# One layer of a hybrid decoder on one core: the opening projection unit with one root per pair of row tiles, and its weight split, scaling, products and clearing in a new order

## The chip, the cores and the metric

The kernel runs on one core of a Trainium2 chip. Its engines work side by side, each through its own instructions in order: PE (TensorE, matrix products), with PEld for its weight loads, DVE (VectorE), ACT (ScalarE), POOL (GpSimd) and SP, which here only issues DMAs. The metric is the device time of one execution in microseconds (us), lower is better. Times of a trace are counted from the start of the profiled span.

## The reference, cut to what matters

```python
def reference(x, mem, ...):
    h = rms_norm(x, attn_norm[l])          # x: 512 rows of 1024, each divided by its root mean square
    proj = h @ w_in[l]                     # split into q, k, v, RWKV columns, memory q
    o_da = diff_attention(...)
    o_rw = rwkv7_time_mix(...)
    o_mem = memory_attention(...)
    x = x + concatenate([o_da, o_rw, o_mem]) @ w_out[l]
    xn = rms_norm(x, ffn_norm[l])
    return x + hierarchical_moe(xn, ...)   # 16 experts, two for each row

def rms_norm(x, gain, eps=1e-6):
    return x * rsqrt(mean(x * x, axis=-1, keepdims=True) + eps) * gain
```

The change touches only `rms_norm(x)` and the first 256 columns of `h @ w_in` (the LoRA columns of the RWKV group).

## The kernel before, in words

The 512 rows of x lie in four tiles of 128 rows, `xt[0]` to `xt[3]`; the first two are the halves of one buffer (`f_96` in lists of the order, `f` in the trace), the last two of another (`f_97`). The opening is done in two halves `hf` of 256 rows, one pair of tiles each:

- *Roots.* `row_root` sums a tile's squares for each row, on DVE (line 280, for tiles 0 and 2) or on ACT (line 282, for tiles 1 and 3; the sum is read out by a second short instruction), then POOL takes mean plus epsilon (line 283) and the power -1/2 (line 284). The squares themselves go to the scratch tiles `aw0` and `aw1`.
- *Scaling.* `half_scale` multiplies the pair by its roots: ACT takes the even tile in two pieces of 512 columns (line 355), DVE the odd one (line 356).
- *Transposes.* `half_turn(n)` turns block k of 128 columns of both tiles on PE into half of a PSUM bank (line 329). There are 16, n = 0 to 7 for the first half. Banks are shared: n = 6 and 7 use the second halves of the banks of n = 0 and 1.
- *Splits.* `half_split(n)` makes of the turned block a rounded part `hm_h` on ACT (line 292) and the remainder `hm_l` on DVE (line 293).
- *Weights.* The 256 columns come in two slots of 512 KB, `raw_79` and `raw_82`. `weights()` lets the next one be split in the same way: `whi` on ACT (line 97), `wlo` on DVE (line 98).
- *Products.* `half_products(hf, ks)` does for each block k and each of two column groups three products of 256 columns: `hm_h` by `whi`, `hm_l` by `whi`, `hm_h` by `wlo` (lines 342 to 344). A half has 48.

ACT, DVE and PE run these in the order in which the code stands (`manual_schedule`). POOL and SP do not: a scheduler places their instructions. What must not come early is put behind `later()`, which ties it to the instruction `rooted`: the clearing of a scratch tile and its DMA into spare rows of the output (lines 394, 395; the scratch tile is `aw1` again), and the clearing of `v_t`, `gm` and a mask `ob` (lines 414, 568, 584). POOL also computes distances of positions (line 897 on), for which SP loads two lists, `pown` and `posc`. After the unit PE goes on with `cols_unit`, the next projections.

Of the kernel before, what the change touches and what calls it, by code (L numbers as in the profile page):

```python
# [10 lines left out]
F32 = mybir.dt.float32  # L11
# [3 lines left out]
AF = mybir.ActivationFunctionType  # L15
ALU = mybir.AluOpType
# [4 lines left out]
P = 128  # L21
S = 512
D = 1024
NT = S // P
KC = D // P
# [6 lines left out]
RMS_EPS = 1e-6  # L32
# [119 lines left out]
def hybrid_layer_kernel(ctx, tc, x, mem, positions, cols, w_in, w_kv, w_out, wa2, g2, ffn, wr, br,  # L152
                        wg, wu, wd, out):
    nc = tc.nc
    V, A, G, T = nc.vector, nc.scalar, nc.gpsimd, nc.tensor
# [4 lines left out]
    wk = ctx.enter_context(tc.tile_pool(name="wk", bufs=2))  # L160
# [14 lines left out]
    def pc():  # L175
        return pools["ps"].tile([P, 512], F32, name="pc", bufs=2)
# [18 lines left out]
    def b4(name, shape, dtype=F32):  # L195
        return biga.tile(shape, dtype, name=name)
# [4 lines left out]
    xt = [xs[t // 2][:, t % 2, :] for t in range(NT)]  # L201
# [36 lines left out]
    mhalf = const.tile([P, 1], F32, name="mhalf")  # L238
# [31 lines left out]
    h_hi = hm.tile([P, KC, S], F32R, name="hm_h")  # L270
    h_lo = hm.tile([P, KC, S], F32R, name="hm_l")
# [4 lines left out]
    def row_root(src, vec=True):  # L276
        ss = wk.tile([P, 1], F32, name="ssx", bufs=4)
        r = wk.tile([P, 1], F32, name="rsx", bufs=4)
        if vec:
            V.tensor_tensor_reduce(b4("aw0", [P, D]), src, src, 1.0, 0.0, op0=ALU.mult, op1=ALU.add, accum_out=ss)  # L280
        else:
            A.activation(b4("aw1", [P, D]), src, AF.Square, accum_out=ss)
        G.tensor_scalar(r, ss, 1.0 / D, RMS_EPS, op0=ALU.mult, op1=ALU.add)
        return r, G.tensor_tensor(r, r, mhalf, op=ALU.pow)

    def row_scale(src):
        r, rooted = row_root(src)
        A.activation(src, src, AF.Copy, scale=r)
        return rooted

    def split_cols(ps, g, hi, lo):
        first = A.activation(hi, ps, AF.Copy, scale=g)
        return first, V.scalar_tensor_tensor(lo, ps, g, hi.bitcast(F32), op0=ALU.mult, op1=ALU.subtract)
# [19 lines left out]
    def weights():  # L313
        ws.pair.append(held.pop())
        ws.pump()
        first_w.append(ws.use())
# [3 lines left out]
    def half_bank(n):  # L320
        if n % 12 < 6 and len(banks) <= n // 12 * 6 + n % 6:
            banks.append((pt, pt, pc, pc, pp, pp)[n % 6]())
        return banks[n // 12 * 6 + n % 6][:, n % 12 // 6 * 256:n % 12 // 6 * 256 + 256]

    def half_turn(n):
        hf, k = divmod(n, KC)
        o = half_bank(n)
        for t in range(2):
            T.transpose(o[:, t * P:(t + 1) * P], xt[2 * hf + t][:, k * P:(k + 1) * P], ident)

    def half_split(n):
        hf, k = divmod(n, KC)
        tk = slice(hf * 256, hf * 256 + 256)
        return split_cols(half_bank(n), col[:, C_AN + k:C_AN + k + 1], h_hi[:, k, tk], h_lo[:, k, tk])

    def half_products(hf, ks):
        tk = slice(hf * 256, hf * 256 + 256)
        for k in ks:
            hi, lo = first_w[k // 4]
            for j in range(2):  # L340
                o, wh, wl = first_ps[j][:, tk], hi[:, k % 4, j * P:(j + 1) * P], lo[:, k % 4, j * P:(j + 1) * P]
                T.matmul(o, wh, h_hi[:, k, tk], start=hf == 0 and k == 0, stop=False, skip_group_check=True)
                T.matmul(o, wh, h_lo[:, k, tk], start=False, stop=False, skip_group_check=True)
                T.matmul(o, wl, h_hi[:, k, tk], start=False, stop=k == KC - 1, skip_group_check=True)

    with tc.manual_schedule(engines={mybir.EngineType.Activation, mybir.EngineType.DVE, mybir.EngineType.PE}):
        early = pc()
        for _ in range(80):
            T.matmul(early[:, 0:P], onb, onb, start=True, stop=True)
        roots = [row_root(xt[0]), row_root(xt[1], False)]  # L350

        def half_scale(hf):
            for i in range(2):
                cs = slice(i * 512, i * 512 + 512)
                A.activation(xt[2 * hf][:, cs], xt[2 * hf][:, cs], AF.Copy, scale=roots[2 * hf][0])
                V.tensor_scalar(xt[2 * hf + 1][:, cs], xt[2 * hf + 1][:, cs], roots[2 * hf + 1][0], None, op0=ALU.mult)

        half_scale(0)
        for n in range(6):
            half_turn(n)  # L360
        weights()
        for n in range(2):
            half_split(n)
        for n in (6, 7):
            half_turn(n)
        for n in range(2, 4):
            half_split(n)
        roots += [row_root(xt[2]), row_root(xt[3], False)]
        weights()
        half_products(0, range(4))  # L370
        for n in range(4, KC):
            half_split(n)
        half_scale(1)
        half_products(0, range(4, KC))
        for n in range(KC, KC + 4):
            half_turn(n)
        half_split(KC)
        half_split(KC + 1)
        for n in range(KC + 4, 2 * KC):
            half_turn(n)  # L380
        for n in range(KC + 2, 2 * KC):
            got_h = half_split(n)
        half_products(1, range(KC))
    rooted = roots[3][1]
    ws.pair.extend(reversed(held))
    with tc.issue_after(got_h[0].ins), tc.issue_after(got_h[1].ins):
        ws.cool()
# [123 lines left out]
    def norm_mem():  # L511
        with tc.issue_after(got_h[0].ins), tc.issue_after(got_h[1].ins):
            for t in range(2):
                row_scale(m_sb[:, t, :])
        yield 5.0
        for k in range(0, KC, 2):
            ps = pt()
            for i in range(2):
                for t in range(2):
                    T.transpose(ps[:, i * M + t * P:i * M + (t + 1) * P], m_sb[:, t, (k + i) * P:(k + i + 1) * P], ident)  # L520
            for i in range(2):
                split_cols(ps[:, i * M:(i + 1) * M], col[:, C_MN + k + i:C_MN + k + i + 1], m_hi[:, k + i, :],
                           m_lo[:, k + i, :])
            yield 2.0
        flags.add("mem")
# [382 lines left out]
    def attention():  # L908
# [79 lines left out]
        def values(i):  # L988
            kind, h, qb = units[i]
            pr, sm = st.pop(i)  # L990
            if kind == "d":
                ob = obs[h % 2]
                po = pt()
                for kb in range(qb + 1):
                    T.matmul(po[:, 0:P], aws[i % 2][:, kb * P:(kb + 1) * P], qk["v"][:, kb, h * P:(h + 1) * P],  # L995
                             start=kb == 0, stop=kb == qb)
                A.activation(ob[:, qb * P:(qb + 1) * P], po[:, 0:P], AF.Copy, scale=sm[:, 2:3])
                if qb < NT - 1:
                    return None
                osq = aws[h % 2][:, 512:1024]  # L1000
                ss = wk.tile([P, 4], F32, name="sso")
                A.activation(osq, ob, AF.Square)
                V.tensor_reduce(ss, osq.rearrange("p (t n) -> p t n", t=4), axis=AX.X, op=ALU.add)
                r = rsqrt(wk, ss, 4, 1.0 / P, RMS_EPS, "o", wide=True)
                V.tensor_mul(ob.rearrange("p (t n) -> p t n", t=4), ob.rearrange("p (t n) -> p t n", t=4),
                             r[:, :, None].to_broadcast([P, 4, P]))

                def close():
                    mix_hi, mix_lo = mix["hi"], mix["lo"]
                    ps = pt()  # L1010
                    for t in range(NT):
                        T.transpose(ps[:, t * P:(t + 1) * P], ob[:, t * P:(t + 1) * P], ident)
                    split_cols(ps, ext[:, E_SUB:E_SUB + 1], mix_hi[:, h, :], mix_lo[:, h, :])
                    flags.add(f"m{h}")
                return close
# [241 lines left out]
    for z in ORDER.split():  # L1257
        op, t = z[0], int(z[1:] or 0)
# [254 lines left out]
```

## Time and profile before

| what | value |
|---|---|
| median of 3 runs | 619.9 us (619.77 to 620.21) |
| the profiled execution's own time | 619.01 us |
| its span in the trace | 617.3 us |
| mean granted TensorE clock | 0.993 |
| PE busy | 599.2 us (97%) |
| DVE, ACT, POOL busy | 500.5, 415.8, 125.5 us |

The span runs from the first to the last instruction; the execution's own time holds 1.7 us more, around it. The profiled execution is 0.9 us below the median of the three runs. Matmuls are pipelined, so a busy PE does not have to be a PE at its peak.

### The profile page before, as it was taken

Reading aid. Unit: us, or ns where it says so; the run is one execution under the profiler, and the core shown is the slowest. Engines: PE = TensorE matmul, PEld = TensorE weight load, DVE = VectorE, ACT = ScalarE, POOL = GpSimd, SP = SyncE. Lnnn points to the kernel's source line nnn. Section 1 sums busy time; section 2 is a strip of 40 time slices with the busy share of each in tenths; the row PEclk is TensorE's granted clock in tenths of the full one; section 3 lists DMA queues with packets and bytes.
Section 4 is the critical chain, followed back from the end, with each engine's and each line's share of the span. In section 5 each row is a group of like instructions: output and inputs, shape, how many; then the busy total and the mean of one; then the engine's idle time right before and its main releaser. Section 6 shows DMA issues by size and latency. Waiting matters only on the chain.

```text
span 617.3 us, 11297 instructions
## 1 busy us (share of the span) xinstructions
PE 599.2 (97%) x4178; PEld 484.4 (78%) x4178; DVE 500.5 (81%) x899; ACT 415.8 (67%) x635; POOL 125.5 (20%) x129
## 2 busy tenths in 40 slices
PE   7999999999999999999999999999999999999992
PEld 7968899999988777989986776777777777777771
DVE  5965976799846688666488999999999999988991
ACT  6488343544458776564337788888887988888880
POOL 3901011334400232223020111111100111410001
PEclk9999999999999999999999999999999999999997
DMA  9542243322342008896999999999999999799813
GB/s 304 179 121 69 89 137 86 104 68 70 99 91 71 1 3 294 284 339 213 341 299 343 364 345 365 361 372 369 368 353 357 368 360 364 229 378 374 331 27 55
DMA packets 77504, 144.21 MB, mean 234 GB/s; under 512 B 12833, under 2 KB 30497, under 8 KB 77441
## 3 DMA queue, kind: packets, MB, share of 16 engines
q1 hardware_dynamic: 69344, 126.59, 58.5%
q0 software_dynamic: 3760, 13.24, 9.1%
q10 hardware_dynamic: 4336, 3.57, 1.9%
q8 instruction: 35, 0.57, 0.4%
q14 instruction: 29, 0.23, 0.1%
HBM read 131.72 MB, written 11.67 MB: 232 GB/s over the span
## 4 chain that ended last, share of the span: by engine, by line
PE 90%; DVE 5%; DMA 2%; ACT 1%; issue 1%; POOL 0%; POOLq 0%; DVEq 0%; ACTq 0%
PE pp L244 18%; PE pp L246 17%; PE pp L245 17%; PE py L245 5%; PE py L246 4%; PE py L244 4%; PE pp L1073 2%; DVE wlo L98 2%; PE pp L1075 2%; PE pp L1074 2%; PE pt L995 2%; PE pp L1355 2%; PE py L1211 1%; PE pc L688 1%; PE pl L1178 1%
## 5 line engine op out<-in xcount | busy, mean ns | idle before, releaser
L246 PE MATMUL pp<-whi,xl 128*96 128x512 f32 x264 | 104.1, 395 | 0.0
L245 PE MATMUL pp<-wlo,xh 128*96 128x512 f32 x264 | 103.8, 394 | 0.0
L244 PE MATMUL pp<-whi,xh 128*96 128x512 f32 x264 | 101.2, 394 | 0.8 <-ACT xh L1342 0.8
L1403 POOL DMA_INDIRECT out<-ye,sidx x16 | 23.2, 1452 | 226.4 <-DVE gidx L1305 133.8
L244 PE MATMUL pp<-whi,hm_h 128*128 128x256 f32 x224 | 64.4, 288 | 0.0
L98 DVE TENSOR_TENSOR wlo<-raw,whi 128x1024 fp32r<-128x1024 f32 x42 | 52.3, 1253 | 13.8 <-ACT whi L97 13.4
L246 PE MATMUL pp<-whi,hm_l 128*128 128x256 f32 x224 | 63.2, 282 | 0.0
L97 ACT ACTIVATE whi<-raw 128x1024 fp32r<-128x1024 f32 x42 | 44.2, 1060 | 27.7 <-PE pp L246 19.1
L245 PE MATMUL pp<-wlo,hm_h 128*128 128x256 f32 x224 | 62.4, 278 | 0.0
L244 PEld LDWEIGHTS pp<-whi,xh 128*96 128x96 f32 x264 | 42.5, 161 | 19.6 <-ACT xh L1342 1.3
L246 PEld LDWEIGHTS pp<-whi,xl 128*96 128x96 f32 x264 | 42.6, 161 | 18.4
L245 PEld LDWEIGHTS pp<-wlo,xh 128*96 128x96 f32 x264 | 42.5, 161 | 18.2
L245 PE MATMUL py<-wlo,hh 128*96 128x512 f32 x120 | 47.9, 399 | 0.0
L246 PE MATMUL py<-whi,hl 128*96 128x512 f32 x120 | 47.0, 392 | 0.0
L244 PE MATMUL py<-whi,hh 128*96 128x512 f32 x120 | 47.0, 392 | 0.0
L98 DVE TENSOR_TENSOR wlo<-lraw,whi 128x1024 fp32r<-128x1024 f32 x36 | 42.6, 1218 | 2.7 <-ACT whi L97 2.7
L98 DVE TENSOR_TENSOR wlo<-u,whi 128x1024 fp32r<-128x1024 f32 x34 | 41.6, 1252 | 3.0 <-ACT whi L97 2.9
L244 PEld LDWEIGHTS pp<-whi,hm_h 128*128 128x128 f32 x224 | 42.1, 188 | 2.0 <-issue 0.7
L246 PEld LDWEIGHTS pp<-whi,hm_l 128*128 128x128 f32 x224 | 42.2, 188 | 0.6 <-issue 0.2
L245 PEld LDWEIGHTS pp<-wlo,hm_h 128*128 128x128 f32 x224 | 42.1, 188 | 0.4 <-issue 0.2
L97 ACT ACTIVATE whi<-lraw 128x1024 fp32r<-128x1024 f32 x36 | 37.1, 1058 | 5.1 <-PE pp L246 3.6
L97 ACT ACTIVATE whi<-u 128x1024 fp32r<-128x1024 f32 x34 | 35.0, 1056 | 3.0 <-PE pp L246 2.2
(407 smaller groups left out, 1564.9 us busy)
## 6 DMA issues: line engine op xcount, KB each, us to landing
raw<-in_w_in SPq DMA_DIRECT2D x22, 512.0 KB
lraw<-in_wg SPq DMA_DIRECT2D x12, 512.0 KB
lraw<-in_wu SPq DMA_DIRECT2D x12, 512.0 KB
lraw<-in_wd SPq DMA_DIRECT2D x12, 512.0 KB
u<-in_wd SPq DMA_DIRECT2D x12, 512.0 KB
f<-in_wg SPq DMA_DIRECT2D x11, 512.0 KB
u<-in_wu SPq DMA_DIRECT2D x11, 512.0 KB
eraw<-in_wd SPq DMA_DIRECT2D x10, 512.0 KB
```

The lines of the kernel that those rows point to most:

```text
L97: nc.scalar.activation(hi, slot, AF.Copy)
L98: nc.vector.tensor_sub(lo, slot, hi.bitcast(F32))
L244: T.matmul(ps, ah, bh, start=first, stop=False)
L245: T.matmul(ps, ah, bl, start=False, stop=False)
L246: T.matmul(ps, al, bh, start=False, stop=last)
L688: paired([lambda h=h, q=q: T.matmul(pq[q][:, h * P:(h + 1) * P], bk[sr(q), ci, h], u1[sr(q), q, ci, h], start=True, stop=True) for h in ra ...
L995: T.matmul(po[:, 0:P], aws[i % 2][:, kb * P:(kb + 1) * P], qk["v"][:, kb, h * P:(h + 1) * P], start=kb == 0, stop=kb == qb)
L1073: T.matmul(o, ah, hi[:, k % 4, :], start=k == k0 and i == lead, stop=False, skip_group_check=True)
L1074: T.matmul(o, ah, lo[:, k % 4, :], start=False, stop=False, skip_group_check=True)
L1075: T.matmul(o, al, hi[:, k % 4, :], start=False, stop=k == k1, skip_group_check=True)
L1355: T.transpose(ps[:, k * CAP:(k + 1) * CAP], xg[:, (b * 4 + k) * P:(b * 4 + k + 1) * P], ident[0:CAP, 0:CAP])
L1403: G.indirect_dma_start(out, bass.IndirectOffsetOnAxis(ap=si, axis=0), ye, None, compute_op=ALU.add)
```

## The change

`two_roots(a, b)` replaces two calls of `row_root`: the sums of both tiles of a pair lie in one tile of two columns, and POOL does one mean and one power for both. The first weight's split on ACT stands ahead of ACT's scaling of tile 0, the products of blocks 0 and 1 ahead of transposes 6 and 7, with those by `wlo` last. The second pair's roots are taken after splits 4 and 5, no longer ahead of the second weight, and the scaling of that pair stands behind the first half's last products. `rooted` is now the last scaling instruction on DVE, no longer the last power on POOL.

```diff
+    def two_roots(a, b):
+        ss = wk.tile([P, 2], F32, name="ss2", bufs=2)
+        r = wk.tile([P, 2], F32, name="rs2", bufs=2)
+        V.tensor_tensor_reduce(b4("aw0", [P, D]), a, a, 1.0, 0.0, op0=ALU.mult, op1=ALU.add, accum_out=ss[:, 0:1])
+        A.activation(b4("aw1", [P, D]), b, AF.Square, accum_out=ss[:, 1:2])
+        G.tensor_scalar(r, ss, 1.0 / D, RMS_EPS, op0=ALU.mult, op1=ALU.add)
+        return r, G.tensor_tensor(r, r, mhalf.to_broadcast([P, 2]), op=ALU.pow)
...
-        roots = [row_root(xt[0]), row_root(xt[1], False)]
+        roots = [two_roots(xt[0], xt[1])]
...
-        half_scale(0)
+        half_scale(0, "v")
+        weights()
+        half_scale(0, "a")
         for n in range(6):
             half_turn(n)
-        weights()
-        for n in range(2):
-            half_split(n)
+        half_split(0)
+        half_split(1)
+        half_products(0, (0, 1), "h")
+        half_split(2)
+        half_split(3)
+        half_products(0, (0, 1), "l")
         for n in (6, 7):
             half_turn(n)
-        for n in range(2, 4):
-            half_split(n)
-        roots += [row_root(xt[2]), row_root(xt[3], False)]
+        half_products(0, (2, 3))
         weights()
-        half_products(0, range(4))
-        for n in range(4, KC):
-            half_split(n)
-        half_scale(1)
+        half_split(4)
+        half_split(5)
+        roots.append(two_roots(xt[2], xt[3]))
+        half_split(6)
+        half_split(7)
         half_products(0, range(4, KC))
+        rooted = half_scale(1)
...
-    rooted = roots[3][1]
```

How this moves instructions is seen on ACT first, from the first sum of squares to the second half's scaling. Before, with the split of weight `raw_79` behind the scaling of `f_96`:

```order
L282 ACTIVATE aw_227,ssx<-f_96 128x1024
L355 ACTIVATE f_96<-f_96,rsx 128x512 x2
L97 ACTIVATE whi_80<-raw_79 128x1024
L292 ACTIVATE hm_h<-pt,col 128x256 x2
L292 ACTIVATE hm_h<-pc,col 128x256 x2
L282 ACTIVATE aw_276,ssx<-f_97 128x1024
L97 ACTIVATE whi_83<-raw_82 128x1024
L292 ACTIVATE hm_h<-pp,col 128x256 x2
L292 ACTIVATE hm_h<-pt,col 128x256 x2
L355 ACTIVATE f_97<-f_97,rsx 128x512 x2
```

and on the same engine and stretch with the change (line 295 is the sum of squares, 368 the scaling, 300 the split of a block):

```order
L295 ACTIVATE aw_223,ss_219<-f_96 128x1024
L97 ACTIVATE whi_80<-raw_79 128x1024
L368 ACTIVATE f_96<-f_96,rs_220 128x512 x2
L300 ACTIVATE hm_h<-pt,col 128x256 x2
L300 ACTIVATE hm_h<-pc,col 128x256 x2
L97 ACTIVATE whi_83<-raw_82 128x1024
L300 ACTIVATE hm_h<-pp,col 128x256 x2
L295 ACTIVATE aw_299,ss_295<-f_97 128x1024
L300 ACTIVATE hm_h<-pt,col 128x256 x2
L368 ACTIVATE f_97<-f_97,rs_296 128x512 x2
```

The first weight's split went ahead of the scaling, and the second pair's sum of squares went behind the second weight's split and two block splits. On POOL, from the second root of the first pair to the first operation on positions, before (what a row waits for stands in brackets):

```order
L283 TENSOR_SCALAR rsx<-ssx 128x1 [waits Activation_49]
L284 TENSOR_TENSOR rsx<-rsx,mhalf 128x1 [waits Pool_49]
L283 TENSOR_SCALAR rsx<-ssx 128x1 [waits DVE_49]
L283 TENSOR_SCALAR rsx<-ssx 128x1 [waits Activation_49]
L284 TENSOR_TENSOR rsx<-rsx,mhalf 128x1 [waits Pool_49] x2
L394 MEMSET aw_440 128x1024
L414 MEMSET v_t 128x2x64
L568 MEMSET gm 128x128
L584 MEMSET ob_471 128x512
L395 DMA out<-aw_440 128x1024 [waits Pool_49]
L897 TENSOR_TENSOR pown<-posc,pown 128x128 [waits DMAHW2_49,DMAHW1_49]
```

and with the change, from the first pair's joint root on (lines 296 and 297 are mean and power, 413 and 414 the clearing and its DMA, 916 and 917 the positions):

```order
L296 TENSOR_SCALAR rs_220<-ss_219 128x2 [waits DVE_49,Activation_49]
L297 TENSOR_TENSOR rs_220<-rs_220,mhalf 128x2 [waits Pool_49]
L413 MEMSET aw_432 128x1024 [waits Activation_49]
L414 DMA out<-aw_432 128x1024 [waits Pool_49]
L296 TENSOR_SCALAR rs_296<-ss_295 128x2 [waits DVE_49]
L916 TENSOR_TENSOR pown<-posc,pown 128x128 [waits DMAHW2_49,DMAHW1_49]
L297 TENSOR_TENSOR rs_296<-rs_296,mhalf 128x2 [waits Pool_49]
L917 CAST dist<-pown 128x128 [waits Pool_49]
```

The clearing of `aw`, its DMA and the first operation on positions now stand ahead of the second pair's power, where they stood behind it; the clearings of `v_t`, `gm` and `ob` stand among POOL's first instructions, ahead of all roots.

Behind this unit, PE, DVE and ACT have some of the small operations of the next projections (transposes of `kT`, products of `ths`) a few rows earlier or later; SP's order is the same.

## Rows read from the trace of the kernel before

**Rows 1.** The page's chain that ended last, by engine.

```profile
PE 90%; DVE 5%; DMA 2%; ACT 1%; issue 1%; POOL 0%; POOLq 0%; DVEq 0%; ACTq 0%
```

**Rows 2.** Busy time by stretch: length, PE, PEld, DVE, ACT, POOL, clock, DMA, GB/s.

```profile
7.60:12.20 4.60, 2.29 (x16) 1.67 (x16) 3.44 (x10) 4.38 (x8) 0.79 (x3) 1.00 1.05 402
12.20:18.30 6.10, 6.03 (x50) 5.82 (x50) 6.10 (x10) 4.25 (x9) 4.13 (x9) 1.00 0.89 232
```

**Rows 3.** Timeline of PE: start, length, operation, [idle before, releaser].

```profile
9.13 0.55 PE L329 MATMUL pt<-ident,f 128*128 128x128 f32 x3 [0.36 <-DVE f L356]
...
18.33 0.74 PE L329 MATMUL pc<-ident,f 128*128 128x128 f32 x4
...
20.53 0.36 PE L342 MATMUL pp<-hm_h,whi 128*128 128x256 f32 x1
```

**Rows 4.** Timeline of ACT, 5 to 19 us.

```profile
5.78 1.06 ACT L282 ACTIVATE aw<-f 128x1024 f32<-128x1024 f32 x1 [3.69 <-DMA f<-in_x]
6.74 0.19 ACT L282 ACTIVATION_READ_ACCUMULATOR aw<-f 128x1 f32 x1
7.67 1.34 ACT L355 ACTIVATE f<-f,rsx 128x512 f32<-128x512 f32 x2 [0.74 <-POOL rsx L284]
8.91 1.04 ACT L97 ACTIVATE whi<-raw 128x1024 fp32r<-128x1024 f32 x1
9.86 0.82 ACT L292 ACTIVATE hm_h<-pt,col 128x256 fp32r<-128x256 f32 x2
...
12.61 1.05 ACT L97 ACTIVATE whi<-raw 128x1024 fp32r<-128x1024 f32 x1
...
16.05 1.34 ACT L355 ACTIVATE f<-f,rsx 128x512 f32<-128x512 f32 x2 [0.94 <-POOL rsx L284]
18.89 0.84 ACT L292 ACTIVATE hm_h<-pc,col 128x256 fp32r<-128x256 f32 x2 [1.50 <-PE pc L329]
```

**Rows 5.** Timeline of DVE, 8 to 19 us.

```profile
8.59 0.88 DVE L356 TENSOR_SCALAR f<-f,rsx 128x512 f32<-128x512 f32 x2 [1.49 <-POOL rsx L284]
...
9.99 1.23 DVE L98 TENSOR_TENSOR wlo<-raw,whi 128x1024 fp32r<-128x1024 f32 x1 [0.16 <-ACT whi L97]
11.13 0.87 DVE L293 SCALAR_TENSOR_TENSOR hm_l<-pt,col,hm_h 128x256 fp32r<-128x256 f32 x2
...
12.70 1.22 DVE L280 CUSTOM_DVE_ANT_0 aw<-f 128x1024 f32<-128x1024 f32 x1
...
16.57 2.44 DVE L356 TENSOR_SCALAR f<-f,rsx 128x512 f32<-128x512 f32 x2
```

**Rows 6.** Timeline of POOL, 7 to 20 us.

```profile
7.06 0.58 POOL L284 TENSOR_TENSOR rsx<-rsx,mhalf 128x1 f32<-128x1 f32 x1
...
14.01 1.37 POOL L283 TENSOR_SCALAR rsx<-ssx 128x1 f32<-128x1 f32 x2 [5.45 <-DVE ssx L280]
...
16.48 0.96 POOL L394 MEMSET aw<- 128x1024 f32 x1
...
18.14 0.99 POOL L395 DMA_DIRECT2D out<-aw  x1
19.16 0.41 POOL L897 TENSOR_TENSOR pown<-posc,pown 128x128 int32<-128x128 int32 x1
```

**Rows 7.** Groups of POOL over the whole span: powers of four columns, with their mean.

```profile
L261 POOL TENSOR_TENSOR rs_yo<-rs_vo,mhalf 128x4 f32<-128x4 f32 x4 | 4.0, 1010 | 22.4 <-DVE rs_vo L259 22.4
```

**Rows 8.** SP's queue, 5 to 9 us: an issue on the timeline; its wait (total, times, longest).

```profile
7.43 0.38 SPq L309 DMA_DIRECT2D posc<-in_positions  x1
...
SPq L309 <- DMA raw<-in_w_in: 1.2, 1, 1.2
```

**Rows 9.** DMA packets by size, 16.4 to 16.8 us.

```profile
DMA packets 129, 0.12 MB, mean 289 GB/s; under 512 B 16, under 2 KB 129, under 8 KB 129
```

**Rows 10.** Timelines of DVE and POOL around 65 us.

```profile
64.26 1.41 DVE L699 SCALAR_TENSOR_TENSOR r_t<-r_t,col,k_t 128x512 f32<-128x512 f32 x2
...
64.80 0.53 POOL L721 MEMSET lor<- 128x512 f32 x1 [6.06 <-PE pc L651]
```

More of the change, by code (lines that the diff above doesn't have):

```diff
@@ L334, in half_split, with half_products @@
         return split_cols(half_bank(n), col[:, C_AN + k:C_AN + k + 1], h_hi[:, k, tk], h_lo[:, k, tk])
-    def half_products(hf, ks):
+    def half_products(hf, ks, parts="hl"):
         tk = slice(hf * 256, hf * 256 + 256)
@@ L341, in half_products @@
                 o, wh, wl = first_ps[j][:, tk], hi[:, k % 4, j * P:(j + 1) * P], lo[:, k % 4, j * P:(j + 1) * P]
-                T.matmul(o, wh, h_hi[:, k, tk], start=hf == 0 and k == 0, stop=False, skip_group_check=True)
-                T.matmul(o, wh, h_lo[:, k, tk], start=False, stop=False, skip_group_check=True)
-                T.matmul(o, wl, h_hi[:, k, tk], start=False, stop=k == KC - 1, skip_group_check=True)
+                if "h" in parts:
+                    T.matmul(o, wh, h_hi[:, k, tk], start=hf == 0 and k == 0, stop=False, skip_group_check=True)
+                    T.matmul(o, wh, h_lo[:, k, tk], start=False, stop=False, skip_group_check=True)
+                if "l" in parts:
+                    T.matmul(o, wl, h_hi[:, k, tk], start=False, stop=k == KC - 1, skip_group_check=True)
     with tc.manual_schedule(engines={mybir.EngineType.Activation, mybir.EngineType.DVE, mybir.EngineType.PE}):
@@ L349, in hybrid_layer_kernel, with half_scale @@
             T.matmul(early[:, 0:P], onb, onb, start=True, stop=True)
-        roots = [row_root(xt[0]), row_root(xt[1], False)]
-        def half_scale(hf):
+        roots = [two_roots(xt[0], xt[1])]
+        def half_scale(hf, on="av"):
+            scaled = None
             for i in range(2):
                 cs = slice(i * 512, i * 512 + 512)
-                A.activation(xt[2 * hf][:, cs], xt[2 * hf][:, cs], AF.Copy, scale=roots[2 * hf][0])
-                V.tensor_scalar(xt[2 * hf + 1][:, cs], xt[2 * hf + 1][:, cs], roots[2 * hf + 1][0], None, op0=ALU.mult)
-        half_scale(0)
+                r = roots[hf][0]
+                if "a" in on:
+                    A.activation(xt[2 * hf][:, cs], xt[2 * hf][:, cs], AF.Copy, scale=r[:, 0:1])
+                if "v" in on:
+                    scaled = V.tensor_scalar(xt[2 * hf + 1][:, cs], xt[2 * hf + 1][:, cs], r[:, 1:2], None, op0=ALU.mult)
+            return scaled
+        half_scale(0, "v")
+        weights()
+        half_scale(0, "a")
         for n in range(6):
             half_turn(n)
-        weights()
-        for n in range(2):
-            half_split(n)
+        half_split(0)
[4 more added lines that the diff above has]
+        half_products(0, (0, 1), "l")
         for n in (6, 7):
             half_turn(n)
-        for n in range(2, 4):
-            half_split(n)
-        roots += [row_root(xt[2]), row_root(xt[3], False)]
+        half_products(0, (2, 3))
         weights()
-        half_products(0, range(4))
-        for n in range(4, KC):
-            half_split(n)
-        half_scale(1)
+        half_split(4)
[3 more added lines that the diff above has]
+        half_split(7)
         half_products(0, range(4, KC))
+        rooted = half_scale(1)
         for n in range(KC, KC + 4):
```

## The prediction

> **What bounds the kernel now.** The chain that ended last comes first: it is on PE for 90% of the span [rows 1]. What is saved or lost in the opening therefore moves the end by as much, as long as PE behind it runs without gaps. Busy time by stretch comes next: between 7.6 and 12.2 us PE is busy for 2.29 of 4.60 us and waits; from 12.2 to 18.3 it is full, with 50 matmuls in 6.10 us, 0.12 us each [rows 2]. So there are two places to look at, and PE's timeline shows what ends each. The first half's transposes run in earnest from 9.13, when DVE's scaling has come [rows 3]. The second half's begin at 18.33 and its products at 20.53 [rows 3]; ACT had then waited 1.50 us for PE, so PE's own first half set that start [rows 4]. The whole change is worth what it does to the start of the second half's products, 20.53 us.
>
> **First half, roots and scaling.** The joint root needs both sums; ACT's is read out at 6.74 + 0.19 = 6.93 [rows 4]. I allow 0.4 us for the hand-over and the mean, so the power starts at 7.33. A power of one column takes 0.58, of four 1.01 [rows 6, 7]; two lie between, and on the line through both take 0.72: ready at 8.05. DVE scales from 8.08 where it did at 8.59, and two pieces take 0.88 [rows 5]. ACT now splits the first weight ahead of its scaling, and must wait for that weight. SP's issue at 7.43 waited for that weight's DMA [rows 8], so it had landed by then. The split starts at 7.45, the next operation 0.95 later (8.91 to 9.86), and the scaling at 8.40, where it was 7.67 [rows 4]. Its first piece ends about 9.12. The transposes start when the later of both engines is done: 9.15 against 9.13. Here the change earns nothing; the wait goes from DVE to ACT.
>
> **First half, splits and products.** ACT reaches the first block split at 8.40 + 1.24 = 9.64 (two scalings took 7.67 to 8.91), against 9.86. Four splits, one each 0.36 us (two in 0.82 with a 0.1 overlap), end by 11.1. The second weight's split begins there, not at 12.61, because the second pair's sum of squares has left its way: 1.5 us earlier [rows 4]. On DVE the first weight's remainder starts at 9.2 against 9.99; block remainders follow 1.14 later, from 10.34 against 11.13, one each 0.39 [rows 5]. The second weight's remainder starts when ACT is through, at 11.1 + 1.05 + 0.03 = 12.18; blocks 4 and 5 follow at 13.32 and 13.71, the sum of squares at 14.10 takes 1.14 (12.70 less the overlap), and blocks 6 and 7 come out at 15.7 and 16.1. PE has the first remainder at 10.8, is through products and transposes up to block 3 at 13.9 (24 products of 0.12 and four transposes, which are no longer than a product, from 10.4 on with short waits), does blocks 4 and 5 by 15.3, waits 0.4 for block 6, and ends the first half at 17.0, against 18.33. Alone that would be 1.3 us.
>
> **Second half: where it is given back.** The order shows what has become of "clearing later". `rooted` is now an instruction of DVE, and POOL has the clearing of `aw`, its DMA and a position operation ahead of the second power. The clearing writes the scratch tile that ACT's second sum of squares uses, so POOL stands until that sum is out: ACT 11.1 + 0.95 + 0.72 = 12.77 for its start, read out 0.96 to 1.15 later, 13.92. Then follow the clearing, 14.0 to 14.96 (0.96), its DMA's issue, to 16.0 (0.99), and the mean, to 16.2. The position operation takes 0.41 [rows 6] and waits for both position lists. Their landing has no row. They are among the small packets, of which 16 under 512 B still pass between 16.4 and 16.8 [rows 9]; the lists were issued ahead of two other small loads, so I take 16.3. Earlier than 16.2 would change nothing, since POOL is not there before; the end of that window, 16.8, would add 0.5. The power then runs from 16.75 to 17.5. ACT scales from 17.53, where it began at 16.05, and gives the first turned block's split at 18.77, against 18.89 [rows 4]. PE's 1.3 us turn into a wait of that size for these tiles.
>
> DVE's scaling of this pair took 2.44 us before, 0.88 in the first half [rows 5]: it began at 16.57, when POOL's clearings had begun at 16.48 [rows 6]. These clearings are gone from there, but POOL's conversion and mask of 128 positions follow the power at once. If each delays a piece of DVE's by no more than the position operation's 0.41, the two pieces are done 1.7 us after the power at the latest; ACT's take 1.34, and the second piece is wanted only for blocks 12 to 15. I count nothing as gained or lost here. DVE's multiplication of the router weights now stands ahead of that scaling and can hold the power back by its own length: 160 columns, where 1024 take 1.23 [rows 5], so some 0.2, with its start-up 0.35 at most.
>
> **The sum.** Second half's products start at 20.53 - 0.12 if nothing touches the power, + 0.25 if the router weights do: I take + 0.1. The trace's own execution, 617.3 us in the span and 1.7 around it, goes from 619.0 to 619.1. The median shown is 0.9 above that execution, so the forecast is 619.9 + 0.1 = **620.0 us**. The clearings of `v_t`, `gm` and `ob` cost nothing: at the start POOL idles until the roots at 7.0; at 16.5 they would have cost DVE 1.6. The 512 KB of zeros start their way about 3 us earlier, at 15 instead of 18.14 [rows 6], beside the third and fourth weight pieces, whose splits stand behind all of the second half's block splits (from 18.89 on). The small operations placed otherwise in the next projections stand a few products off: 0 taken, four products of 0.12 (0.5 us) either way.
>
> **Rivals.** *POOL is later still (slower).* The clearing at 14.0 meets DVE's sum of squares at 14.1. At 14.01 POOL's mean, on one column, came under DVE's weight remainder, and two such took 1.37, longer than two whole powers of 0.58 [rows 6]. If the clearing must wait likewise until 15.3, everything up to the power is 1.25 us later: 621.2. It decides when POOL's mean starts after 17 us. Against it: a clearing of 0.53 us ran its usual length at 64.80 in the middle of DVE operations with two inputs from SBUF [rows 10]. The Trainium skill, "SBUF — State Buffer", on the port pair that DVE and GpSimd share, would have it that an operation in a two-port mode, or a GpSimd operation, holds the pair until it ends, and that one of DVE with two SBUF inputs stands only against a GpSimd operation that reads SBUF. By that rule the clearing passes, and the sum above stays; the delay of rows 6 is of an operation that reads. Position lists a good microsecond later than I take them would do the same. I give this 0.15.
>
> *POOL's second power is not late (faster).* If the clearing, its DMA and the positions did stand behind it, as the change is described, the power would follow the sum of squares (15.3) directly, end at 16.4, and ACT would scale from 16.5: the split of block 8 at 17.75, 1.15 earlier, 618.8. PE's own 17.0 is the limit, 618.6. The order speaks against it: 0.07.
>
> *The clock falls (slower).* PE idles now from 7.6 to 9.15 in one piece, and about 1.2 us before 18.2. Before, it was idle for half of 7.6 to 12.2 and the granted clock stayed 1.00, the upper of its levels, 2.4 GHz [rows 2]. If it fell to 1.2 GHz for 3 us of products, that would cost 1.5 or more: 621.5. 0.04.
>
> **How the numbers follow.** About 0.2%, 1.24 us, is what a measurement of this kernel can tell from no change. The main case has 0.74; its own range goes from 619.4 (short power, early lists, 0.3 from the next projections) to 620.8 (a power of 1.01, the router weights, late operations behind). The faster rival ends between 618.6 and 619.2 and passes the bound in half of its cases; the slower ones pass it in most. Faster 0.06, within the bound 0.79, slower 0.15. For eight in ten the range runs from 619.1 to 621.2.
>
> **What the changed profile would show.** ACT's weight split from about 7.45 and scaling at 8.4; first transposes still near 9.15; second weight's split near 11.1; the first half's last product near 17.0, then an idle PE ended by ACT's or DVE's scaling; on POOL the clearing at 14.0 and the second power near 16.8; the second half's first product near 20.6. The forecast is wrong if POOL's power comes before 16 or after 18, if the first weight lands late, or if PE has new gaps in the projections behind the unit.

## The result, and the profile after

The kernel with the change takes 624.54 us (median of 4 runs, 624.21 to 624.73), the one before 619.84 in the same comparison: ratio 1.007, 95% interval 1.0055 to 1.0084. It is 4.7 us slower. The forecast was 620.0, its range ended at 621.2.

The page of the kernel after, its parts 1 and 4 (busy us, share of the span, instructions; the chain that ended last):

```profile
PE 603.5 (97%) x4178; PEld 486.8 (78%) x4178; DVE 498.7 (80%) x899; ACT 416.4 (67%) x635; POOL 122.2 (20%) x125
...
PE 89%; DVE 4%; DMA 2%; ACT 2%; issue 1%; POOL 0%; SPq 0%; DVEq 0%; ACTq 0%; POOLq 0%
```

PE still makes the chain, and this line holds most of the answer already: the same 4178 matmul records keep PE busy for 603.5 us, where they kept it for 599.2 before. Of the 5.2 us between the two profiled spans, 4.3 are longer busy time for the same products and 0.9 longer waits, half of these in the opening; from 26 to 200 us PE has no gap in either kernel. The mean granted clock is 0.995 (0.993 before), so it is not the clock.

The opening itself came out as forecast. ACT's timeline, to be held against [rows 4]:

```profile
7.66 1.06 ACT L97 ACTIVATE whi<-raw 128x1024 fp32r<-128x1024 f32 x1 [0.49 <-DMA raw<-in_w_in]
8.62 1.32 ACT L368 ACTIVATE f<-f,rs 128x512 f32<-128x512 f32 x2
...
11.30 1.08 ACT L97 ACTIVATE whi<-raw 128x1024 fp32r<-128x1024 f32 x1
...
17.91 1.34 ACT L368 ACTIVATE f<-f,rs 128x512 f32<-128x512 f32 x2 [3.04 <-POOL rs L297]
```

POOL's, to be held against [rows 6]:

```profile
14.20 0.95 POOL L413 MEMSET aw<- 128x1024 f32 x1 [5.94 <-ACT aw L295]
15.48 0.84 POOL L414 DMA_DIRECT2D out<-aw  x1 [0.33 <-POOL aw L413]
16.39 0.19 POOL L296 TENSOR_SCALAR rs<-ss 128x2 f32<-128x2 f32 x1
16.66 0.53 POOL L916 TENSOR_TENSOR pown<-posc,pown 128x128 int32<-128x128 int32 x1
17.16 0.72 POOL L297 TENSOR_TENSOR rs<-rs,mhalf 128x2 f32<-128x2 f32 x1
```

DVE's two rows that stand beside these:

```profile
14.34 1.22 DVE L294 CUSTOM_DVE_ANT_0 aw<-f 128x1024 f32<-128x1024 f32 x1
...
17.91 0.93 DVE L370 TENSOR_SCALAR f<-f,rs 128x512 f32<-128x512 f32 x2 [0.98 <-POOL rs L297]
```

and PE's, to be held against [rows 3]; the last row is the first product of the next projection:

```profile
9.38 0.65 PE L337 MATMUL pt<-ident,f 128*128 128x128 f32 x4 [1.70 <-ACT f L368]
...
18.69 0.66 PE L337 MATMUL pc<-ident,f 128*128 128x128 f32 x4 [1.14 <-ACT f L368]
...
20.80 0.37 PE L351 MATMUL pp<-hm_h,whi 128*128 128x256 f32 x1
...
26.36 0.39 PE L244 MATMUL pp<-hm_h,whi 128*128 128x512 f32 x1
```

In the kernel before, that product's row is

```profile
26.27 0.40 PE L244 MATMUL pp<-hm_h,whi 128*128 128x512 f32 x1
```

so the unit ends 0.09 us later, and 0.1 was forecast. The loss lies behind it, in code that the change does not touch: counted by PE's records in order, the kernel after is 0.1 us late at 26 us, 1.8 at 80, 4.0 at 200 and 5.1 at 595. (That is more than 4.7, since the profiled execution before is 0.9 below its median.) Two differences are to be seen there.

**One pair of products comes apart.** At 35 us a unit multiplies the two 64-row halves of `ths` (line 618 before, 637 after), as pairs, the second product of a pair tied behind the first by the code. There are two such pairs; the second, from 40 us on, is apart in both kernels. PE's timeline of the first, before:

```profile
35.06 1.13 PE L618 MATMUL pc<-ths,prod 64*128 64x512 f32 x4
```

its group of these products from 30 to 48 us (busy us, mean ns):

```profile
L618 PE MATMUL pc<-ths,prod 64*128 64x512 f32 x8 | 3.4, 641 | 0.0
```

The same two views after:

```profile
34.49 1.12 PE L637 MATMUL pc<-ths,prod 64*128 64x512 f32 x2
...
35.97 1.12 PE L637 MATMUL pc<-ths,prod 64*128 64x512 f32 x2
```

```profile
L637 PE MATMUL pc<-ths,prod 64*128 64x512 f32 x8 | 4.5, 641 | 0.0
```

Each product has two records. Before, the two products of the first pair ran together, four records in 1.13 us, as long as two take alone. After, a product of the projection stands between them, they run one after the other, and the eight records need 4.5 us instead of 3.4.

**The same products have another pace.** Two products of one dense stream (256 columns, `hm` by weights), 48 products apart, before (a start is read to 0.01 us, so a pace to some 0.2 ns):

```profile
101.92 0.28 PE L245 MATMUL pp<-wlo,hm_h 128*128 128x256 f32 x1
...
107.36 0.28 PE L245 MATMUL pp<-wlo,hm_h 128*128 128x256 f32 x1
```

and after:

```profile
104.11 0.28 PE L245 MATMUL pp<-wlo,hm_h 128*128 128x256 f32 x1
...
109.76 0.28 PE L245 MATMUL pp<-wlo,hm_h 128*128 128x256 f32 x1
```

That is 5.44 / 48 = 113.3 ns from product to product before and 5.65 / 48 = 117.7 after; nothing waits in either, and the length of a row, 0.28, is the same. The granted clock is 1.00 in both, the upper level, 2.4 GHz.

### The profile page after: what moved, and what is told of

The parts are those of the page before. It is cut to its first block, busy times and chain, and to the rows that moved or that the text cites. A ratio compares the mean times of both kernels' runs of the same rounds, so it can differ in the third digit from the quotient of the medians.

```text
span 622.5 us, 11290 instructions
## 1 busy us (share of the span) xinstructions
PE 603.5 (97%) x4178; PEld 486.8 (78%) x4178; DVE 498.7 (80%) x899; ACT 416.4 (67%) x635; POOL 122.2 (20%) x125
## 4 chain that ended last, share of the span: by engine, by line
PE 89%; DVE 4%; DMA 2%; ACT 2%; issue 1%; POOL 0%; SPq 0%; DVEq 0%; ACTq 0%; POOLq 0%
PE pp L244 18%; PE pp L246 17%; PE pp L245 17%; PE py L245 5%; PE py L246 4%; PE py L244 4%; PE pp L1092 2%; PE pp L1094 2%; PE pp L1093 2%; PE pt L1014 2%; DVE wlo L98 2%; PE pp L1374 1%; PE py L1230 1%; DMA raw<-in_w_in 1%; PE pc L707 1%
```

## The experiments

Three theories were set against each other. *Opening*: the loss comes from the unit, its roots and POOL's queue. *Order*: it comes from the other order behind the unit. *Pace*: the streams fall into one pace or another, and any shift in time can decide which.

**First four: undo the parts.** Which instructions stand where behind the unit turned out to hang on what `later()` is tied to, so the kernel before with the tie moved has the whole order of after there:

```diff
-                V.tensor_scalar(xt[2 * hf + 1][:, cs], xt[2 * hf + 1][:, cs], roots[2 * hf + 1][0], None, op0=ALU.mult)
+                scaled = V.tensor_scalar(xt[2 * hf + 1][:, cs], xt[2 * hf + 1][:, cs], roots[2 * hf + 1][0], None, op0=ALU.mult)
+            return scaled
...
-        half_scale(1)
+        rooted = half_scale(1)
...
-    rooted = roots[3][1]
```

> The kernel before with one edit: the later clearings are tied to the last scaling on DVE, no longer to POOL's last power. Its opening unit is that of before; behind the unit every engine has the order of the kernel after. Theory order (the 4.6 us come from where the small operations of the next projections stand): 624 to 625 us. Theory opening (they come from the unit itself, its roots and POOL's queue): 619.5 to 620.5. Theory pace (the dense streams of products on PE fall into one of two paces, 113 or 118 ns for 256 columns, and any small shift ahead of them can decide which): anywhere from 619 to 625, and the time goes with the number of streams at 118 between 80 and 200 us.

Measured: 621.83 us against 620.01, ratio 1.0029 (1.002 to 1.0038). The group of `ths` products has after's busy time:

```profile
L618 PE MATMUL pc<-ths,prod 64*128 64x512 f32 x8 | 4.5, 641 | 0.0
```

The order costs something, but under half of the loss: theory order and theory opening both miss. The stream at 102 us keeps before's pace, 113 ns. The other way round, the kernel after with before's order, by two of its clearings (`v_t` and `gm`), in front of both of which this line is changed:

```diff
+    def early_enough():
+        return tc.issue_after(roots[1][1].ins)
...
-    with later():
+    with early_enough():
```

> The kernel after with the clearing of v_t and of the mask gm tied to POOL's second power; the clearing of aw stays tied to DVE. The unit is that of after, with POOL's second power late as there; behind the unit the order is that of before but for one transpose of kT. Theory order: 619.5 to 620.5 us. Theory opening: 624 to 625. Theory pace: anywhere from 619 to 625, with the streams at 118 ns as its measure.

Measured: 623.12 us, ratio 1.0048 (1.0036 to 1.006). The order is mended (`ths` again 3.4 us), most of the loss stays, and the stream has 118 ns. Theory order (619.5 to 620.5) falls as the whole cause. The third ties everything to POOL's power, which lets the power run early:

```diff
-        rooted = half_scale(1)
+        half_scale(1)
...
+    rooted = roots[1][1]
```

> The kernel after with all later clearings tied to POOL's second power, as before. POOL's second power then stands ahead of the clearing of aw, so ACT should scale the second pair near 16.5 us, not at 17.9, and the unit should end about 1.1 us earlier. The order behind the unit is a third one, about as far from before's as from after's. Theory opening: 618.5 to 619.5 us. Theory order: no forecast but that it differs from both by whole microseconds. Theory pace: 618 to 624, by its streams.

Measured: 624.65 us, ratio 1.0067 (1.0054 to 1.008). Its `ths` products are apart too (34.36 and 35.84), and its stream has 118 ns. From its timelines of POOL, DVE and PE:

```profile
15.95 0.71 POOL L297 TENSOR_TENSOR rs<-rs,mhalf 128x2 f32<-128x2 f32 x1
16.60 0.98 POOL L415 MEMSET aw<- 128x1024 f32 x1
...
16.93 2.22 DVE L370 TENSOR_SCALAR f<-f,rs 128x512 f32<-128x512 f32 x2
...
18.67 0.55 PE L337 MATMUL pc<-ident,f 128*128 128x128 f32 x3 [0.86 <-DVE f L370]
```

The power is 1.2 us earlier and nothing comes of it: POOL's clearings then lie beside DVE's scaling, which takes 2.22 us instead of 0.93, and PE starts at 18.67, after at 18.69. The 618.5 to 619.5 of theory opening do not come. The fourth shifts everything behind the unit by one transpose and leaves every place as it is:

```diff
             T.transpose(o[:, t * P:(t + 1) * P], xt[2 * hf + t][:, k * P:(k + 1) * P], ident)
+        if n == 14:
+            T.transpose(o[:, P:2 * P], xt[2 * hf + 1][:, k * P:(k + 1) * P], ident)
```

> The kernel before with the second transpose of block 14 of the unit done twice (the same result written twice); no other instruction changes its place on any engine. PE is busy there, so the unit ends 0.06 to 0.15 us later. Theory order and theory opening: 620.0 us, at most 0.2 above before. Theory pace: some streams of products behind it take the other pace, and the time differs from before's by more than 1 us, up or down.

Measured: 620.5 us, ratio 1.0007 (0.9998 to 1.0016): nothing that can be told from no change, and its stream has 113.3 ns. So a shift in time does not decide the pace, and theory pace falls in that form. What after, the second and the third kernel, all at 118 ns, share and the others lack is not an order but `two_roots`: its tiles `ss2` and `rs2`, two buffers each, are 128 bytes more in the pool `wk`, since each takes 32. The lists of the compiled programs show what follows (byte in each partition):

```
            before   after
ss2            -     10112
raw0        11680    11808
whi0        15776    15904
f1          52640    52768
v_da       122272   122400
hm_h       196576   196576
hm_l       212960   212960
```

Everything allotted behind `wk` moves by 128 bytes, the weight slots first of all; `hm` comes from the other end and stays. That is a fourth theory, *address*.

**Next four: the address alone.** One tile of before is made 128 bytes larger, and no instruction changes its place. (The edit leaves `rnk` one buffer of two; by itself that costs nothing, as the run moved by 256 bytes shows further down.)

```diff
-        rn = wk.tile([P, 16], F32, name="rnk")
+        rn = wk.tile([P, 64], F32, name="rnk", bufs=1)[:, 0:16]
```

> The kernel before with one small tile (rnk) allotted 128 bytes more in each partition; every instruction and its place on every engine is that of before, but all tiles that are allotted behind it, the weight slots among them, stand 128 bytes further on in SBUF, as they do in the kernel after (its new tiles ss2 and rs2 take 4 times 32 bytes). The tiles hm_h and hm_l stay where they are. Theory address (the pace of the products, 113 or 118 ns for 256 columns, goes with where the operands lie in SBUF): 622.5 to 623.5 us, as much above before as the kernel with after's unit and before's order behind it, and the streams of products between 80 and 180 us at 118 ns. Rival opening (the pace is carried over from how the unit ends in time): 620.0, no change.

Measured: 623.39 us against 619.77, ratio 1.0062 (1.0048 to 1.0075). Two products of the stream, 48 apart:

```profile
103.00 0.28 PE L245 MATMUL pp<-wlo,hm_h 128*128 128x256 f32 x1
...
108.66 0.28 PE L245 MATMUL pp<-wlo,hm_h 128*128 128x256 f32 x1
```

and part 1 of its page:

```profile
PE 602.7 (97%) x4178; PEld 486.4 (78%) x4178; DVE 500.5 (81%) x899; ACT 415.8 (67%) x635; POOL 123.9 (20%) x129
```

5.66 / 48 = 117.9 ns: after's pace and 3.6 us, by an edit that adds not one instruction. And after with the bytes taken back:

```diff
-        ss = wk.tile([P, 1], F32, name="ssx", bufs=4)
-        r = wk.tile([P, 1], F32, name="rsx", bufs=4)
+        ss = wk.tile([P, 1], F32, name="ssx", bufs=2)
+        r = wk.tile([P, 1], F32, name="rsx", bufs=2)
```

> The kernel after with two buffers less of the small tiles ssx and rsx (2 where it has 4 of each), which takes back the 128 bytes: the tiles behind stand where they stand in before. No instruction changes its place. Theory address: the pace part is gone and the order behind the unit stays: 621.5 to 622.3 us, as the kernel before with after's order behind the unit. Rival opening: 624.5, no change.

Measured: 621.07 us, ratio 1.0024 (1.0015 to 1.0033), with before's pace in that stream:

```profile
103.33 0.28 PE L245 MATMUL pp<-wlo,hm_h 128*128 128x256 f32 x1
...
108.77 0.28 PE L245 MATMUL pp<-wlo,hm_h 128*128 128x256 f32 x1
```

A second profile of the kernel of the second run (after's unit and addresses, before's order) was to show whether the pace repeats:

> A second profile of the kernel with after's unit, before's order behind it and the addresses of after: the same as at its first run, 622.7 to 623.8 us, with the streams of products at 118 ns. It serves to see whether the pace repeats from one execution to the next.

Measured: 623.80 us, one run; the stream again at 117.9 ns (102.95 to 108.61). It repeats. The last of the four joins the edits of the second and the sixth run, and only the unit of after is left:

> The kernel after with the clearings of v_t and gm tied to POOL's second power (before's order behind the unit) and with the 128 bytes taken back (before's addresses). What is left of the change is the unit itself. Theory address and order together: 620.0 to 620.3 us, within 0.2 of before, which is what the forecast said of the unit. Rival opening: 623.

Measured: 620.03 us, ratio 1.0001 (0.9992 to 1.001). Theory opening falls: the unit's worth cannot be told from nothing (-0.5 to 0.6 us by the interval), and 0.1 was forecast.

**Then: which addresses.** The same padding with other sizes, and twice `hm` moved instead (its pool grows downwards; here by 128 bytes):

```diff
-    h_lo = hm.tile([P, KC, S], F32R, name="hm_l")
+    h_lo = hm.tile([P, KC * S + 32], F32R, name="hm_l")[:, 0:KC * S].rearrange("p (k s) -> p k s", k=KC)
```

> The kernel before, all tiles behind rnk 64 bytes further on (128 gave 3.6 us). No instruction moves. Theory half (what decides is a step between 0 and 128 bytes): either 619.8 or 623.4 us. Theory graded (the loss grows with the distance): about 621.6.

> The kernel before, all tiles behind rnk 256 bytes further on. No instruction moves. If what decides repeats every 256 bytes: 619.8 us, streams at 113 ns as before. If it repeats every 512 or more: another time, 617 to 624, and one below 619 would show that before's own addresses were not the best.

> The kernel before, all tiles behind rnk 384 bytes further on. No instruction moves. Period 256: 623.4 us, as with 128. Period 512: another time than both.

> The kernel before with hm_h and hm_l 128 bytes further down and everything else in the attention part where it is; the distance between the weight slots and hm is then that of the run moved by 128. No instruction moves. Theory distance (what counts is how the two operands of a product lie to each other): the streams between 80 and 300 us at 118 ns, and about the 2.9 us that were lost up to 300 us, so 622.7; the expert part, whose products do not use hm, as before. Theory slots (what counts is where the weight slots lie): 619.8.

> The kernel before, all tiles behind rnk 192 bytes further on: weight slots and hm are 128 bytes apart, modulo 256. No instruction moves. Theory distance: a time of its own; if the pace gets better the further the operands are from distance 0 (120 ns at 0, 118 at 64, 113 at 192), 113 ns or less in all streams from 80 to 300 us, 617 to 619.9 us. Theory slots: no forecast.

> The kernel before with hm_h and hm_l 192 bytes further down, the weight slots where they are: again 128 bytes apart. No instruction moves. Theory distance: the streams from 80 to 300 us at the pace of the run with the slots moved by 192, whatever that is. Theory slots: 113 ns as in before, 619.9 us.

> The kernel before, all tiles behind rnk 32 bytes further on: distance 224. No instruction moves. If only a distance very near to 0 is bad, 113 ns and 619.9 us; if the pace falls off with the distance to 0 on either side, between 113 and 120 ns and 621 to 623 us.

> The kernel before, all tiles behind rnk 224 bytes further on: distance 160 between weight slots and hm. No instruction moves. 192 gave 113 ns, 128 and 224 gave 118 to 119 and 3.5 to 4.4 us: if only 192 is good (half a period of a step of 64 would make 32 off bad), 623 to 624.5 us; if the good distances are a range from 160 to 192, 620 or less.

> The kernel before, all tiles behind rnk 160 bytes further on: distance 96. No instruction moves. 64 gave 118 and 128 gave 119 ns: 623 to 624.5 us.

All together, ordered by the distance of the weight slots from `hm` (whi0 less hm_h, modulo 256). The pace is that of the stream shown above, from two starts 48 products apart:

| moved, bytes | distance | pace, ns | median, us | ratio to before (95%) |
|---|---|---|---|---|
| none (before) | 192 | 113.3 | 619.8 to 620.2 in six comparisons | 1 |
| slots 256 | 192 | 113.3 | 619.68 | 0.9998 (0.9988 to 1.0008) |
| slots 224 | 160 | 118.8 | 624.00 | 1.0064 (1.0049 to 1.008) |
| slots 192 | 128 | 118.8 | 623.56 | 1.0055 (1.0038 to 1.0072) |
| hm 192 | 128 | 118.6 | 623.45 | 1.0066 (1.0042 to 1.0091) |
| slots 160 | 96 | 120.0 | 625.88 | 1.0091 (1.0075 to 1.0106) |
| slots 128 | 64 | 117.8 | 623.39 | 1.0062 (1.0048 to 1.0075) |
| slots 384 | 64 | 117.8 | 623.02 | 1.0047 (1.0029 to 1.0065) |
| hm 128 | 64 | 117.8 | 621.83 | 1.0031 (1.002 to 1.0041) |
| slots 64 | 0 | 120.0 | 624.23 | 1.0078 (1.0053 to 1.0102) |
| slots 32 | 224 | 118.3 | 624.36 | 1.008 (1.0052 to 1.0108) |

Two of the rows behind it, the stream with the slots moved by 64:

```profile
102.33 0.28 PE L245 MATMUL pp<-wlo,hm_h 128*128 128x256 f32 x1
...
108.09 0.28 PE L245 MATMUL pp<-wlo,hm_h 128*128 128x256 f32 x1
```

What follows: it repeats after 256 bytes (256 is as none, 384 nearly as 128). It goes with the distance of the two operands, not with the slots' own place: moving `hm` by 192 gives the time and pace of moving the slots by 192. For 128 that holds in the stream shown, but in time only by half; some streams kept 113 ns there (8 of the 28 counted under *Open*, 6 with the slots moved), and the expert part, whose products do not use `hm`, kept its time (products at 320 and 595 us start 2.61 and 2.66 us later than the same ones of before; with the slots moved 3.40 and 3.93). Of the distances tried, 192, which before has by accident, is the only one at which most streams of 256 columns ran at 113 ns. The forecasts of a step between 0 and 128 bytes, of an even growth, and of a better pace far from 0 all failed: 64 bytes cost more than 128, distance 128 is no better than 64, and 224 is bad. Distance 96 came out worse than forecast (625.88 us against 623 to 624.5). Every kernel here also holds a second sign of it: the products of `mem` at 72 us have `v_da` and the weight slots as operands, which keep distance 0 in all these programs since they move together. Before:

```profile
71.49 0.28 PE L245 MATMUL pp<-wlo,v_da 128*128 128x256 f32 x1
...
76.53 0.28 PE L245 MATMUL pp<-wlo,v_da 128*128 128x256 f32 x1
```

5.04 / 42 = 120.0 ns, the pace of distance 0 in the table. This stream has 119.9 to 120.0 ns in every kernel of this document, whatever moved.

**Last: the best that these point to.** After's unit, before's order and addresses, and the experts' tiles 192 bytes further down:

> The unit of after with before's order behind it and before's addresses, and the tiles of the expert part moved down by 192 bytes, which brings their products to the distance from the weight slots at which the run moved by 192 won 0.3 us between 320 and 595 us. 619.5 to 620.0 us: not to be told from before, as nothing in the unit was won.

Measured: 619.58 us against 620.15, ratio 0.9991 (0.9982 to 1.0001): not to be told from before, clearly better than after.

## Why the prediction was wrong

**What held.** The steps of the opening came within about 0.5 us, and some 0.2 of that stood at the start already (ACT's first sum of squares begins at 6.01, [rows 4] 5.78). ACT's split came at 7.66 (7.45 forecast), its scaling at 8.62 (8.4), the transposes at 9.38 (9.15), the second weight's split at 11.30 (11.1), the clearing at 14.20 (14.0), POOL's power at 17.16 (16.75), then an idle PE ended by ACT's scaling, and the second half's first product at 20.80 (20.6). That the unit's end then fits the forecast to 0.01 us is luck: its second half starts 0.27 late, and its 48 products run at 113.4 ns where before's ran at 117.8, which gives 0.2 back and was in no sum. The clearing ran its usual 0.95 beside DVE's sum of squares (14.34 to 15.56); by the rule of the Trainium skill's "SBUF — State Buffer" (section on its two separate sides) it passes, and the trace agrees. So the rival with a later POOL falls, and so does the falling clock (1.00 throughout). The faster rival, POOL's power not late, was tried in the third run and was mis-sized: it left out that DVE's scaling then stretches to 2.22 us, which gives PE the same start.

**The step that failed** is the one on what lies behind the unit: "The small operations placed otherwise in the next projections stand a few products off: 0 taken, four products of 0.12 (0.5 us) either way." The order cost 1.82 us by itself (first run) and 1.0 on top of the new unit (sixth run less eighth). About 1.1 us of PE's time is the one pair of `ths` products: 4.5 less 3.4 us. The moved operations were priced by their own length and place, not by what they do to those beside them: one product put between two others cost as much as nine products of 0.12. The compiled order shows it, PE's rows around the pair, before and then after:

```
L244 MATMUL pp<-hm_h,whi_87 128x512
L618 MATMUL pc<-ths,prod 128x512 x2

L637 MATMUL pc<-ths,prod 128x512
L245 MATMUL pp<-hm_l,whi_87 128x512
L637 MATMUL pc<-ths,prod 128x512
```

**The step that was missing** is larger: nothing in the sum spoke of the 128 bytes of `ss2` and `rs2`. The prediction carried the unit's gain or loss to the end "as long as PE behind it runs without gaps". From 26 to 200 us PE has no gap in either kernel, and the one after loses 3.9 us there all the same: each product behind the unit was taken to cost what it cost before, and 2.9 us (second run, less the unit's 0.3) to 3.6 us (fifth) came from just that. Counting instructions could not find it: the fifth run has before's instructions in before's order.

The parts add up within their spread: unit 0.3 (eighth run less before), order 1.0 to 1.8, addresses 2.9 to 3.6; together 4.2 to 5.7, measured 4.7. They need not add exactly, since what the addresses cost may depend on the order. The page's busy time of PE, always 4178 records, tells the same in one number per kernel: 598.3 us for the unit alone, 599.2 before, 600.5 with after's order, 602.7 with after's addresses, 603.5 after. The run moved by 256 bytes, whose time is before's, has 598.4, so a difference under 1 us says nothing.

**Open.** Why a distance modulo 256 bytes sets the pace is not shown. Nor does the distance say all. Of 28 streams of at least 14 products of 256 columns in a row between 80 and 320 us, before has 23 at 113.3 to 115.3 ns and 5 at 117.8; with the slots moved by 128 bytes, 6 have 113.3 to 113.4 and 22 have 117.7 to 117.9. So at 192 and at 64 both paces occur, and the distance shifts how often. What decides for a single stream was not tested; the instant at which it restarts behind a small operation is a guess.

Which operand lies ahead of the other may count too. At 102 us the stationary operand, which PEld loads, is `hm`, and the weights move; in the opening unit it is the other way round. The unit's second half ran at 117.8 ns in all seven kernels with distance 192, and at 113.4 in three of the seven with 64 (after, the third run, the slots moved by 384). Products of 512 columns follow the distance with less scatter: the stream at 26 us has 228.7 to 229.0 ns in the seven with 192, 233.2 to 233.4 in the seven with 64, and 226.8 at distance 0, the best there and the worst for 256 columns. Distance 32 was not tried on these streams, nor were `v_da` and the slots moved against each other.

## What to carry to other kernels

A new small tile is never only a small tile: it moves all that is allotted behind it, and on a kernel that PE bounds this was worth 2.9 to 3.6 us of 620 here, three fifths to three quarters of what the change cost. Before a change is judged by its time, hold the addresses of the large operands fixed (take the bytes from a pool that has them to spare), and compare PE's busy time at an equal count of records. When a scheduler decides the order, look in it for what has to stay adjacent, and not only for what moved.

## What the runs showed of the hardware

- Dense streams of products of 256 columns ran at 113.3, 117.8, some 118.5 or 120.0 ns each at a granted clock of 1.00, mostly by where their two operands lie to each other modulo 256 bytes. Products of 512 columns ran at 226.8 to 234 ns, likewise. By the Trainium skill, "SBUF — State Buffer" (the section on the bandwidth-pool intuition), PE reads its moving operand on one port and loads weights through a second, independent one. The measured paces do not look like two reads that never touch each other, and the measurement decides; that it is these two reads that meet is not shown.
- Two products of 64 rows ran together when adjacent (four records in 1.13 us) and one after the other when a full product stood between them (two records in 1.12 each). "TensorEngine Tiling (Array Packing)" of the Trainium skill, section on the tiling modes, has tiles work independently; the trace agrees, for neighbours.
- DVE's scaling of 2 x 512 columns took 0.93 us with POOL's conversion and mask beside it (after) and 2.22 with POOL's clearings (third run).
